# Up product of the feed-forward block: a third one of the seven block products leaves out the two leading columns, and its operand starts 32 columns later in its tile

## The chip, the cores and the metric

The kernel runs on one core of a Trainium2 chip. The metric is the device time of one execution in microseconds (us); lower is better. Times are medians of several runs, and beside them stands one profiled execution, from whose trace all durations of single instructions come. The engines are named as in the profile: PE (TensorE, matrix products), PEld (its weight loads), DVE (VectorE), ACT (ScalarE), POOL (GpSimd), SP (SyncE, which issues most DMAs).

## The reference

One decoder layer on 1040 positions (16 meta tokens and 1024 tokens) of width 1024. After attention, a convolution module and a gated merge, the layer normalises and ends with a convolutional feed-forward block. This block is what the change touches:

```python
h = layer_norm(DEEPNORM_ALPHA * h + mixed @ w_out, ln1_g, ln1_b)
up = causal_dwconv(h @ ffn_w_up, ffn_dw, ffn_dw_b)     # 1024 -> 2 * 2816, then 3 taps along the sequence
u, g = jnp.split(up, 2, axis=-1)
f = (jax.nn.gelu(g, approximate=False) * u) @ ffn_w_down
return layer_norm(DEEPNORM_ALPHA * h + f, ln2_g, ln2_b)
```

The three causal taps need two positions ahead of the first token that is put out. The kernel therefore carries 1026 columns: two leading ones, which are the last two meta tokens, and 1024 tokens.

## The kernel before

All products are float32, made of three matmuls on split operands: `hi*hi`, `hi*lo` and `lo*hi`, where `hi` is the operand cast to the PE's type and `lo` the rest. The stages follow one another: input product and attention, merge, output product with the first layer norm, up product, down product with the second layer norm.

The **up product** `h @ ffn_w_up` works on channels in the partitions and sequence positions in the columns. It is cut into 22 chunks of 128 channels of each of the two halves (up and gate), `for c in range(FC)` at L1473. In a chunk a 2 by 2 block product (two halves of the output channels, two halves of the 1024 inputs; two halves of the sequence) is formed with seven block products in place of eight, in the manner of Strassen and Winograd. The seven right-hand operands B11, B21, BT2, BT1, BT3, BT4, B22 are differences of blocks of `h`. They are formed once, split into `hi` and `lo` by `bsplit` (ACT copy L1188, DVE subtraction L1193), and stay in SBUF for all 22 chunks at the places of `B_AT` (tile, first column). The left-hand operands (weights) are split anew for each chunk by `wsplit` (ACT L1315, DVE L1316, with sums and differences on DVE L1333).

Each operand covers one half of the sequence, 512 tokens and two leading columns: `HW = 514` columns, in two sub-blocks `SUB = [(0, 258), (258, 514)]`. Sub-block 1 has 256 columns. Sub-block 0 has 258, of which the first two are the leading ones. `columns(sub, q)` says which columns a product `q` covers; for sub-block 0, BT3 and B22 begin at column 2. An operand's `hi` and `lo` parts are each four blocks (one per 128 inputs) of that many columns, packed one after the other.

`prod(q, bank, first)` at L1485 issues the matmuls of one product (L1497): for each sub-block, four blocks of inputs by three matmuls, so 12 matmuls of 258 or 256 columns. I call these 12 a group. A chunk has 7 products of two groups, 14 groups. In chunk 0 alone the work goes in two passes, all products of sub-block 1 first, then all of sub-block 0. The order on PE is written out: each product is pinned behind the one before (`last_mm`).

The results go to four PSUM tiles of two banks each: X (`px` in the profile), Z (`pz`), V4 (`pw`) and Y (`py`). The order in a chunk and what empties them:

```python
prod(B11, X, True);  copy(u13[:, a:b], at(X))            # ACT L1509
prod(B21, Z, True);  tt(c11[:, a:b], at(Z), u13[:, a:b], OP.add)   # DVE L1505
prod(BT2, X, False); copy(u2[:, a:b], at(X))
prod(BT4, V4, True)
prod(BT1, Y, True);  copy(c22[:, i:b], at(Y, i))          # i = max(a, 2)
prod(BT3, X, False); copy(u13[:, a:b], at(X))
prod(B22, Y, False); tt(c12[:, i:b], at(Y, i), u2[:, i:b], OP.add)
```

BT1 is thus the product that starts Y, and Y is read only from column `i = 2` on (for its two leading columns c22 and c12 take the last two columns of the other half, by the copy at L1544). Behind the evacuations, DVE and ACT run the three taps (L1422 to L1424), the gelu (L1428) and the gating (L1432), and SP stores the result `fd` to DRAM. In most chunks DVE also forms sums for the down product (`sums_form`, L1455 to L1465).

The **down product** (L1635) is a second seven-product scheme. It loads `fd` and weights, splits them (ACT L1594, DVE L1595), and PE takes them in 42 steps, a pair of 128-row blocks at a time.

The order of instructions on ACT, DVE and SP, where it isn't pinned, is set when the program is built, by a scheduler that works with estimated durations and ranks. So an operand that gets shorter can change that order.

Of the kernel before, what the change touches and what calls it, by code (L numbers as in the profile page):

```python
# [101 lines left out]
def tile_hybrid_layer(  # L102
# [41 lines left out]
    RHC = arena.tile([P, 8320], R, name="RHC")  # L144
    RHO = arena.tile([P, 8320], R, name="RHO")
# [768 lines left out]
    OA = oa_p.tile([P, 8320], R, name="OA")  # L914
# [108 lines left out]
    RX = rx_p.tile([P, 2112], R, name="RX")  # L1023
# [115 lines left out]
    def quadrant(sub, kk, h):  # L1139
# [1 line left out]
        return FA[:, h1_at(sub, i):h1_at(sub, i + 4)]  # L1141


    B_AT = [[(RHC, 6224), (RHO, 4112), (OA, 16), (RX, 16), (OA, 2096), (OA, 6224), (OA, 4144)],
            [(OC, 48), (OC, 2096), (OC, 4144), (OC, 6192), (RHC, 2096), (RHC, 48), (RHC, 4144)]]
    B11, B21, BT2, BT1, BT3, BT4, B22 = range(7)

    def columns(sub, q):

        a, b = SUB[sub]  # L1150
        return (2 if q in (BT3, B22) else a) if sub == 0 else a, b

    def bsum(sub, q, hl):
        a, b = columns(sub, q)
        n = b - a
        t, o = B_AT[sub][q]
        return t[:, o + hl * 4 * n:o + (hl + 1) * 4 * n]

    def bmat(sub, q, hl, k):
        a, b = columns(sub, q)  # L1160
        n = b - a
        return bsum(sub, q, hl)[:, k * n:(k + 1) * n]
# [18 lines left out]
    def bsplit(sub, q, src, cs=slice(None)):  # L1181
        with rank(RK_SUMS):
            a = columns(sub, q)[0] - SUB[sub][0]
            x, y, _ = cs.indices(SUB[sub][1] - SUB[sub][0])
            x = max(x, a)
            hi, lo = (wide(bsum(sub, q, hl))[:, :, x - a:y - a] for hl in range(2))
            src = wide(src)[:, :, x:y]
            ins = nc.scalar.copy(hi, src)  # L1188
            if (sub, q) in ((0, BT2), (0, BT4), (0, BT1), (0, BT3)):
                if high:  # L1190
                    after(ins, high[-1])
                high.append(ins)
            line(nc.vector.tensor_tensor(lo, src, f32(hi), OP.subtract))  # L1193
# [279 lines left out]
    for c in range(FC):  # L1473
        V4, X, Z, Y = (pup.tile([P, 1024], F, name=n, tag=n) for n in ("pw", "px", "pz", "py"))
        passes = ((1,), (0,)) if c == 0 else ((0, 1),)
        for subs in passes:
            last = subs == passes[-1]
            w_next = iter(range(7))
            a, b = SUB[subs[0]][0], SUB[subs[-1]][1]
# [310 lines left out]
```

## Time and profile before

| | us |
|---|---|
| median of 3 runs | 1259.55 |
| lowest and highest run | 1259.47, 1259.66 |
| time of the profiled execution | 1259.33 |
| its span in the trace | 1257.1 |
| first and last start of a matmul of the up product (L1497) | 609.0, about 1039 |
| last matmuls of the down product start | 1248.27 |

The span is the time from the first to the last instruction in the trace; 2.2 us of the profiled execution's time lie around it. In an answer that lists instructions by time, a row has the start, the duration of the stretch (for PE with a modelled end, so that stretches overlap), engine, line, operation, `out<-in`, shape and, behind `x`, how many were merged into the row; in brackets stands the idle time before it and what ended that. The time that a group of 12 matmuls really takes is the distance from its start to the start of the next group.

### The profile page before, as it was taken

Reading aid. Unit: us, or ns where it says so; the run is one execution under the profiler, and the core shown is the slowest. Engines: PE = TensorE matmul, PEld = TensorE weight load, DVE = VectorE, ACT = ScalarE, POOL = GpSimd, SP = SyncE. Lnnn points to the kernel's source line nnn. Section 1 sums busy time; section 2 is a strip of 40 time slices with the busy share of each in tenths; the row PEclk is TensorE's granted clock in tenths of the full one; section 3 lists DMA queues with packets and bytes.
Section 4 is the critical chain, followed back from the end, with each engine's and each line's share of the span. In section 5 each row is a group of like instructions: output and inputs, shape, how many; then the busy total and the mean of one; then the engine's idle time right before and its main releaser. Section 6 shows DMA issues by size and latency. Waiting matters only on the chain.

```text
span 1257.1 us, 21713 instructions
## 1 busy us (share of the span) xinstructions
PE 1246.0 (99%) x8546; PEld 1179.2 (94%) x8546; DVE 1086.6 (86%) x1859; ACT 587.4 (47%) x1057; POOL 54.1 (4%) x28
## 2 busy tenths in 40 slices
PE   9999999999999999999999999999999999999997
PEld 8999999999999999788899999999999998888886
DVE  7899989999989587648899999999999986995697
ACT  7522244545474222335565555554555554544330
POOL 0000000010112132000000000000000000000000
PEclk9999999999999999999999999999999999999999
DMA  7294733332155565222145555463464568998722
GB/s 279 73 309 104 192 95 97 106 94 81 68 141 178 155 171 140 77 75 101 68 134 185 193 210 187 184 218 117 154 230 164 203 211 318 390 328 298 249 86 84
DMA packets 96152, 212.10 MB, mean 169 GB/s; under 512 B 10787, under 2 KB 35939, under 8 KB 95922
## 3 DMA queue, kind: packets, MB, share of 16 engines
q1 hardware_dynamic: 84282, 199.64, 47.4%
q10 hardware_dynamic: 11768, 11.08, 2.7%
q8 instruction: 67, 1.10, 0.4%
q14 instruction: 35, 0.29, 0.1%
HBM read 150.29 MB, written 62.70 MB: 169 GB/s over the span
## 4 chain that ended last, share of the span: by engine, by line
PE 96%; ACT 1%; DVE 1%; DMA 0%; issue 0%; ACTq 0%; DVEq 0%; SPq 0%
PE px L1497 14%; PE py L1497 9%; PE ps_x L1635 9%; PE ps_z L305 8%; PE ps_z L301 8%; PE ps_z L306 8%; PE ps_z L1635 7%; PE pz L1497 5%; PE pw L1497 5%; PE ps_p L306 2%; PE ps_p L301 2%; PE ps_p L305 2%; PE ps_w L306 2%; PE ps_w L301 2%; PE ps_w L305 2%; PE ps_z L517 2%
## 5 line engine op out<-in xcount | busy, mean ns | idle before, releaser
L669 DVE SCALAR_TENSOR_TENSOR FA<-cin,cols,FA 128x1026 f32<-128x1026 f32 x120 | 155.2, 1305 | 0.2
L301 PE MATMUL ps_z<-RHO,whi 128*128 128x384 f32 (+2 forms) x324 | 104.7, 323 | 0.2 <-ACT FA L676 0.2
L305 PE MATMUL ps_z<-RHC,whi 128*128 128x384 f32 (+2 forms) x324 | 104.5, 323 | 0.0
L305 PE MATMUL ps_z<-RHO,whi 128*128 128x384 f32 (+2 forms) x324 | 104.0, 321 | 0.0
L306 PE MATMUL ps_z<-RHC,wlo 128*128 128x384 f32 (+2 forms) x324 | 103.7, 320 | 0.0
L301 PE MATMUL ps_z<-RHC,whi 128*128 128x384 f32 (+2 forms) x324 | 103.7, 320 | 0.0
L306 PE MATMUL ps_z<-RHO,wlo 128*128 128x384 f32 (+2 forms) x324 | 103.4, 319 | 0.0
L1316 DVE TENSOR_TENSOR RHO<-wr,RHO 128x512 fp32r<-128x512 f32 x94 | 63.6, 686 | 5.4 <-ACT RHO L1315 5.4
L1315 ACT CAST RHO<-wr 128x512 fp32r<-128x512 f32 x94 | 56.7, 620 | 24.4 <-DVE wr L1333 11.5
L273 ACT CAST whi<-wr 128x1024 fp32r<-128x1024 f32 x37 | 38.9, 1051 | 56.3 <-PE ps_z L305 31.9
L301 PEld LDWEIGHTS ps_z<-RHO,whi 128*128 128x128 f32 x324 | 60.9, 188 | 0.9 <-ACT FA L676 0.4
L305 PEld LDWEIGHTS ps_z<-RHC,whi 128*128 128x128 f32 x324 | 60.9, 188 | 0.4
L306 PEld LDWEIGHTS ps_z<-RHC,wlo 128*128 128x128 f32 x324 | 60.9, 188 | 0.2
L301 PEld LDWEIGHTS ps_z<-RHC,whi 128*128 128x128 f32 x324 | 60.9, 188 | 0.2
L306 PEld LDWEIGHTS ps_z<-RHO,wlo 128*128 128x128 f32 x324 | 61.0, 188 | 0.1
L305 PEld LDWEIGHTS ps_z<-RHO,whi 128*128 128x128 f32 x324 | 60.9, 188 | 0.1
L1333 DVE TENSOR_TENSOR wr<-wr 128x512 f32<-128x512 f32 x88 | 60.3, 685 | 0.2
L276 POOL TENSOR_TENSOR wlo<-wr,whi 128x1024 fp32r<-128x1024 f32 x17 | 42.3, 2488 | 185.3 <-ACT whi L273 175.7
L676 ACT ACTIVATE FA<-ps_z,cols 128x386 f32<-128x386 f32 (+2 forms) x48 | 26.0, 541 | 46.6 <-PE ps_z L306 39.1
L1509 ACT COPY FA<-px 128x514 f32<-128x514 f32 (+2 forms) x23 | 13.1, 571 | 68.0 <-PE px L1497 67.8
L1316 DVE TENSOR_TENSOR ws<-wr,ws 128x512 fp32r<-128x512 f32 x60 | 40.6, 686 | 4.5 <-ACT ws L1315 4.3
L1422 ACT ACTIVATE FA<-OB,cols 128x512 f32<-128x512 f32 x44 | 35.9, 816 | 14.0 <-DVE OB L1505 14.0
(467 smaller groups left out, 3567.3 us busy)
## 6 DMA issues: line engine op xcount, KB each, us to landing
wr<-in_w_up_dram SPq DMA_DIRECT2D x44, 512.0 KB, 4.6
wr<-in_w_z_dram SPq DMA_DIRECT2D x30, 512.0 KB, 4.0
fd<-FA SPq DMA_DIRECT2D x44, 256.0 KB, 2.5
OB<-in_w_down_dram SPq DMA_DIRECT2D x19, 512.0 KB, 6.2
qt<-qd SPq DMA_DIRECT2D x28, 256.0 KB, 3.7
td<-OB SPq DMA_DIRECT2D x12, 512.0 KB
sums<-fd SPq DMA_DIRECT2D x12, 512.0 KB, 4.8
sd<-sums SPq DMA_DIRECT2D x12, 512.0 KB, 2.7
```

Of the source, the lines that this page charges most:

```text
L273: ins = nc.scalar.copy(hi, raw)
L276: return (nc.vector if quick else nc.gpsimd).tensor_tensor(lo, raw, f32(hi), OP.subtract)
L301: ins = nc.tensor.matmul(ps, ah, bh, start=i == 0, stop=False)
L305: nc.tensor.matmul(ps, ah, bl, start=False, stop=False)
L306: last = nc.tensor.matmul(ps, al, bh, start=False, stop=i == n - 1)
L669: nc.vector.scalar_tensor_tensor(acc[c], cin[:, j:j + U], wc, acc[c], OP.mult, OP.add)
L1315: nc.scalar.copy(hi, src)
L1316: ins = nc.vector.tensor_tensor(lo, src, f32(hi), OP.subtract)
L1333: ins = nc.vector.tensor_tensor(*x)
L1422: nc.scalar.activation(t, cc[:, 2:HW], AF.Identity, bias=ffw(3, o), scale=ffw(2, o))
L1497: ins = nc.tensor.matmul(o, x[:, ks], bmat(sub, q, hl, k), start=first and k + j == 0, stop=k == 3 and j == 2, skip_group_check=not first)
L1635: nc.tensor.matmul(banks[i], l[:, ts], r[:, ws], start=first and a and x + k == 0, stop=z and x == len(ops) - 1 and k == 2, skip_group_che ...
```

## The change

`columns` lets BT1 of sub-block 0 begin at column 2 as BT3 and B22 do, and `B_AT` puts that operand at column 48 of the tile RX in place of column 16.

```diff
-    B_AT = [[(RHC, 6224), (RHO, 4112), (OA, 16), (RX, 16), (OA, 2096), (OA, 6224), (OA, 4144)],
+    B_AT = [[(RHC, 6224), (RHO, 4112), (OA, 16), (RX, 48), (OA, 2096), (OA, 6224), (OA, 4144)],
             [(OC, 48), (OC, 2096), (OC, 4144), (OC, 6192), (RHC, 2096), (RHC, 48), (RHC, 4144)]]
     B11, B21, BT2, BT1, BT3, BT4, B22 = range(7)
 
     def columns(sub, q):
 
         a, b = SUB[sub]
-        return (2 if q in (BT3, B22) else a) if sub == 0 else a, b
+        return (2 if q in (BT1, BT3, B22) else a) if sub == 0 else a, b
```

RX has 2112 columns. The operand took columns 16 to 2079 (8 blocks of 258) and takes columns 48 to 2095 (8 blocks of 256). Its 264 matmuls (12 in each of 22 chunks) have 256 moving columns, the cast and the subtraction that make it have 1024 elements in each partition where they had 1032, and the two columns of Y that nobody reads are no longer written.

## The prediction

> **What bounds the kernel now.** I began with the page: the busy times and the chain of work that ended last.
>
> ```profile
> span 1257.1 us, 21713 instructions
> ...
> PE 1246.0 (99%) x8546; PEld 1179.2 (94%) x8546; DVE 1086.6 (86%) x1859; ACT 587.4 (47%) x1057; POOL 54.1 (4%) x28
> ...
> PE 96%; ACT 1%; DVE 1%; DMA 0%; issue 0%; ACTq 0%; DVEq 0%; SPq 0%
> ```
>
> PE is busy for nearly the whole span and makes up 96% of the chain. Next I asked for the waits of PE, and for the busy times from chunk 1 of the up product to the first matmul of the down product (second answer: stretch, its length, then busy time and instructions of PE, PEld, DVE, ACT, POOL, then the granted clock).
>
> ```profile
> PE px L1497 <- ACT OB L1509: 0.3, 1, 0.3
> ```
>
> ```profile
> 631.95:1039.49 407.54, 407.54 (x3530) 407.54 (x3529) 380.83 (x624) 220.27 (x360) 0.00 (x0) 1.00 0.53 187
> ```
>
> In these 407.54 us PE has no gap and the granted clock is 1.00; its wait for an evacuation lies before them, in chunk 0. So the up product is paced by its own stream of matmuls, and what a group costs is the distance between starts. From the timeline of PE alone, one chunk:
>
> ```profile
> 720.75 1.60 PE L1497 MATMUL py<-RX,RHO 128*128 128x258 f32 x12
> 722.19 1.52 PE L1497 MATMUL py<-OC,RHO 128*128 128x256 f32 x12
> 723.55 1.52 PE L1497 MATMUL px<-OA,RHO 128*128 128x256 f32 x12
> 724.91 1.52 PE L1497 MATMUL px<-RHC,RHO 128*128 128x256 f32 x12
> 726.27 1.52 PE L1497 MATMUL py<-OA,RHO 128*128 128x256 f32 x12
> 727.63 1.52 PE L1497 MATMUL py<-RHC,RHO 128*128 128x256 f32 x12
> 728.99 1.59 PE L1497 MATMUL px<-RHC,RHO 128*128 128x258 f32 x12
> 730.42 1.52 PE L1497 MATMUL px<-OC,RHO 128*128 128x256 f32 x12
> ```
>
> The row at 720.75 is BT1 of sub-block 0, the group that the change touches. From 722.19 to 728.99 stand five groups of 256 columns in 6.80 us, 1.360 each. BT1 took 1.44 by these rounded starts. A finer value comes from the whole stretch: 21 chunks in 407.54 us are 19.407 us each; nine groups of 256 take 12.24 of it, and the five of 258 share 7.167, 1.433 each.
>
> **The change part by part.** *The matmuls.* Two columns go from each of these:
>
> ```profile
> L1497 PE MATMUL py<-RX,RHO x156: 277/282/283, 643.1 to 1032.6; 128*128 128x258 f32 x156
> ...
> L1497 PE MATMUL py<-RX,ws x108: 277/282/283, 627.8 to 1013.2; 128*128 128x258 f32 x108
> ```
>
> 156 and 108 are 264 matmuls, 22 groups. What is a group of BT1 worth afterwards? The nearest rows are the two products that already leave the two columns out, BT3 and B22 of sub-block 0 (723.55 and 726.27): 256 columns, packed one block after the other, 1.360. So a group falls from 1.433 by 0.073 us, and 22 groups by 1.6 us. By the rounded starts of the one row (1.44 against 1.36), or by the modelled lengths (1.60 against 1.52), it would be 1.8. At the low end stands the price of two columns alone, from the down product, whose matmuls have 512:
>
> ```profile
> 1039.49 5.62 PE L1635 MATMUL ps_z<-OC,RHC 128*128 128x512 f32 x24
> 1044.95 5.60 PE L1635 MATMUL ps_z<-OC,RX 128*128 128x512 f32 x24
> 1050.39 5.60 PE L1635 MATMUL ps_z<-OC,RHC 128*128 128x512 f32 x24
> ```
>
> From 1044.95 on 24 of them take 5.44 us, 226.7 ns each; a matmul of 256 takes 113.3 (1.360 over 12). That is 0.443 ns a column, and two columns in 264 matmuls would be 0.23 us. But a matmul of 258 takes 119.4 (1.433 over 12), 6 ns over one of 256 where two columns account for 0.9. The trace puts a price on the length of 258, not on the column, and I take 1.6.
>
> The Trainium skill, in "TensorE: Matmul & The Clock Gate", section "Back-to-back issue gap", gives the distance of two warm matmuls as N / 2.4 + 2.5 ns, which charges each column alone: 109.2 ns for 256 and 110.0 for 258, and the change would then bring an estimated 0.2 us. This trace disagrees for these shapes, with 113.3 and 119.4 ns.
>
> *The place.* No row shows an operand of 256 columns read from RX. Rows that come near: with 258 columns RX costs what RHC costs (1.44 at 720.75, 1.43 at 728.99), so the tile itself isn't slower; and the group at 730.42, B11 of sub-block 1, starts at column 48 of its tile and has the 1.52 of all the others. I price the move at nothing; if the place cost what the two columns cost now, the gain would be zero, and I keep that as the upper bound.
>
> *Making the operand.* Once per execution, in chunk 0, the cast and the subtraction have 1024 elements in place of 1032. Rows of the old form and, for BT3 and B22, of the new one, gaps of two columns in the source included:
>
> ```profile
> 622.52 1.06 ACT L1188 CAST RX<-FA 128x1032 fp32r<-128x1032 f32 x1
> 623.48 1.04 ACT L1188 CAST OA<-FA 128x1024 fp32r<-128x1024 f32 x1
> ```
>
> ```profile
> 625.41 1.23 DVE L1193 TENSOR_TENSOR RX<-FA,RX 128x1032 fp32r<-128x1032 f32 x1
> ...
> 627.15 2.35 DVE L1193 TENSOR_TENSOR OA<-FA,OA 128x1024 fp32r<-128x1024 f32 x2
> ```
>
> That is 0.02 us less on ACT and 0.05 on DVE (2.35 over 2 against 1.23). RX is ready at 626.64 and first read at 627.80 (row further down), so on the path it is worth nothing; without that cover it would be a gain of 0.05 at most.
>
> *What is moved.* The order on PE stays. In the order as built, ACT has five single swaps, in chunks 3 to 14, that put an evacuation (L1509) one place earlier, and a sixth, in chunk 14, that puts one behind a tap activation (L1422). In chunks 14 and 15 some 50 DVE rows and a dozen on ACT stand in another order, and SP has two stores of sums ahead of the two stores of `fd` that they stood between; who waits for those stores is the reuse of eight FA buffers and the load of the next sums on DVE. The last six chunks are ordered as before. No wait, no instruction and no DMA is added. What this order can touch on PE is the handover of PSUM: a bank must be copied before PE's next product on it. The tightest of chunks 1 to 21, and a usual one:
>
> ```profile
> 791.70 0.58 ACT L1509 COPY OB<-px 128x514 f32<-128x514 f32 x1
> ...
> 792.79 1.60 PE L1497 MATMUL px<-OA,ws 128*128 128x258 f32 x12
> ```
>
> ```profile
> 1034.31 0.59 ACT L1509 COPY OB<-py 128x512 f32<-128x512 f32 x1
> ...
> 1036.77 1.52 PE L1497 MATMUL py<-OA,RHO 128*128 128x256 f32 x12
> ```
>
> The leads are 0.51 and 1.87 us. What one or two more instructions ahead of a copy cost, from the page:
>
> ```profile
> L1315 ACT CAST RHO<-wr 128x512 fp32r<-128x512 f32 x94 | 56.7, 620 | 24.4 <-DVE wr L1333 11.5
> ...
> L1422 ACT ACTIVATE FA<-OB,cols 128x512 f32<-128x512 f32 x44 | 35.9, 816 | 14.0 <-DVE OB L1505 14.0
> ```
>
> 0.62 and 0.82 together are 1.44, under the usual lead and 0.93 over the tightest: at most 0.9 in each of chunks 14 and 15, at least nothing. I take nothing.
>
> *The seam to the down product.* PE wants the down operands 1.6 us earlier. Of its 42 steps the one with the smallest lead is step 5, which needs the last chunk's `fd`:
>
> ```profile
> 1064.11 0.69 DVE L1595 TENSOR_TENSOR RHO<-OB,RHO 128x512 fp32r<-128x512 f32 x1 [1.16 <-ACT RHO L1594]
> ...
> 1066.71 1.52 PE L1635 MATMUL ps_z<-RHO,RHC 128*128 128x512 f32 x6
> ```
>
> Ready at 1064.80, used at 1066.71: 1.9 us. Even if that chain stayed where it is, 1.6 fits; and it hangs on the last chunk's results, so it moves along. Behind it PE runs on to the end, and the whole 1.6 us should arrive there.
>
> *Sum.* 1259.33 of the profiled execution less 1.6 is 1257.7; its time stands 0.22 under the median, so the median becomes 1259.55 - 1.6 = **1257.9**, 0.13% faster. As no change counts what lies within 0.2%, 1257.0 to 1262.1, about what a measurement can tell.
>
> **The rivals.** *Column price or place* (gain 0.0 to 0.23): the 6 ns belong to something of BT1 other than its length, its tile or its place in the chunk. For it: nothing has tried RX with 256. Against it: 258 columns cost the same from two tiles. Time 1259.3 to 1259.55.
>
> *The gain stops at the seam*: the down operands, bound by their loads, come as late as before or later, and PE waits for them. For it: that lead of 1.9. Against it: it covers 1.6. Time up to 1259.55.
>
> *The slow pace* (slower). The trace has the very same form at two paces. In chunk 0:
>
> ```profile
> 617.00 1.58 PE L1497 MATMUL py<-OC,ws 128*128 128x256 f32 x12
> 618.42 1.58 PE L1497 MATMUL px<-RHC,ws 128*128 128x256 f32 x12
> 619.83 1.58 PE L1497 MATMUL py<-RHC,ws 128*128 128x256 f32 x12
> ...
> 627.80 1.59 PE L1497 MATMUL py<-RX,ws 128*128 128x258 f32 x12
> 629.24 1.52 PE L1497 MATMUL px<-OA,ws 128*128 128x256 f32 x12
> 630.59 1.52 PE L1497 MATMUL py<-OA,ws 128*128 128x256 f32 x12
> ```
>
> 617.00 to 619.83 is 1.415 a group, against 1.35 at 629.24. I cannot name what ends the slow pace. If the changed mix of lengths kept it up, ten groups of 256 in each of 21 chunks would cost 0.055 more, and a chunk 4 x 1.433 + 10 x 1.415 = 19.88: 0.48 over now, 10 us in all, 1269.5. It decides from some 75 groups on (2.5 us for 0.2%, and the 1.6). Against it: the longest run of 256 in a chunk grows from five groups to seven, and within the five no pace changes.
>
> *Larger than summed*: the four other products of 258 columns fall to 1.36 too, because neighbours share what costs 0.073: 88 groups, 6.4 us more, 1251.5. Against it: the row at 728.99 costs 1.43 with groups of 256 on both sides.
>
> *Handover* (slower): the copy comes 0.3 us late in each of 21 chunks (0.82 against the lead of 0.51), 6.3 less 1.6: 1264.3. Five of the six swaps speak against it.
>
> **How the numbers follow.** Forecast 70%; column price or place 6%, seam 4%: these are "same", 80%. Larger 10% is "faster". Slow pace 6% and handover 4% are "slower", 10%. The range reaches from 1257.4 (a gain of 1.8, and 0.2 more each way for the scatter of the runs) to 1259.6 (no gain) and leaves out the last three cases.
>
> **What would show it.** After the change `py<-RX` has 128x256 and its successor starts 1.36 later; a chunk takes 19.33 us; chunk 1 to the first L1635 takes 406.0; PE shows no new wait at L1497 or L1635; from that L1635 to the end it stays 217.6. Wrong would be: a BT1 group over 1.40, groups of 256 at 1.41 in chunks 1 to 21, a wait of PE for L1509, or a down product that grows by what the up product gained.

## The result, and the profile after

| | before | after |
|---|---|---|
| median (22 runs each, same chip), us | 1259.41 | 1257.75 |
| lowest and highest, us | 1259.00, 1259.95 | 1257.46, 1258.85 |
| span of the profiled execution, us | 1257.1 | 1255.5 |
| first matmul of the down product, us | 1039.49 | 1037.93 |

The ratio is 0.9987, with a 95% interval of 0.9981 to 0.9993: 1.66 us less, where 1.6 were forecast. The interval lies below 1, so the gain is clear of the noise; by the prediction's bound of 0.2% it counts as no change.

From the page of the changed kernel, the busy times and the chain that ended last:

```profile
span 1255.5 us, 21717 instructions
...
PE 1244.1 (99%) x8546; PEld 1177.3 (94%) x8546; DVE 1086.5 (87%) x1859; ACT 586.6 (47%) x1057; POOL 54.0 (4%) x28
...
PE 96%; ACT 1%; DVE 1%; DMA 1%; issue 0%; SPq 0%; ACTq 0%; DVEq 0%
```

PE lost 1.9 us of busy time and is still the bound. Next, the waits of PE in the changed kernel (total, times, longest), and its busy times (columns as before) from chunk 1 to the first matmul of the down product and from there to the end:

```profile
PE px L1497 <- ACT OB L1509: 0.4, 1, 0.4
```

```profile
631.93:1037.93 406.00, 406.00 (x3530) 406.00 (x3529) 380.73 (x624) 219.71 (x360) 0.00 (x0) 1.00 0.53 187
1037.93:1255.50 217.57, 209.62 (x926) 173.24 (x924) 172.22 (x247) 81.55 (x92) 0.00 (x0) 0.99 0.69 249
```

The stretch of 21 chunks took 407.54 us and takes 406.00; PE has no gap in it. The down product takes 217.6 as before. So the whole gain is made in the up product and arrives at the end. The timeline of PE in one chunk of the changed kernel:

```profile
701.10 1.52 PE L1497 MATMUL py<-RX,RHO 128*128 128x256 f32 x12
702.46 1.52 PE L1497 MATMUL py<-OC,RHO 128*128 128x256 f32 x12
703.82 1.52 PE L1497 MATMUL px<-OA,RHO 128*128 128x256 f32 x12
705.18 1.52 PE L1497 MATMUL px<-RHC,RHO 128*128 128x256 f32 x12
```

The BT1 group now has 128x256 and its successor starts 1.36 later. Durations of groups are from here on distances of starts in the trace to the nanosecond, in us: BT1 went from 1.434 to 1.360 in each of the 22 chunks, and in chunks 1 to 21 no other group changed by more than 0.001.

So far the sum stands. The diff, however, makes two edits at once, and the prediction gave the whole gain to one of them, the length. The experiments take them apart.

### The profile page after: what moved, and what is told of

It is laid out like the page before. It is cut to its first block, busy times and chain, and to the rows that moved or that the text cites. A ratio compares the mean times of both kernels' runs of the same rounds, so it can differ in the third digit from the quotient of the medians.

```text
span 1255.5 us, 21717 instructions
## 1 busy us (share of the span) xinstructions
PE 1244.1 (99%) x8546; PEld 1177.3 (94%) x8546; DVE 1086.5 (87%) x1859; ACT 586.6 (47%) x1057; POOL 54.0 (4%) x28
## 4 chain that ended last, share of the span: by engine, by line
PE 96%; ACT 1%; DVE 1%; DMA 1%; issue 0%; SPq 0%; ACTq 0%; DVEq 0%
PE px L1497 14%; PE py L1497 9%; PE ps_x L1635 9%; PE ps_z L305 8%; PE ps_z L301 8%; PE ps_z L306 8%; PE ps_z L1635 7%; PE pz L1497 5%; PE pw L1497 5%; PE ps_p L306 2%; PE ps_p L301 2%; PE ps_p L305 2%; PE ps_w L301 2%; PE ps_w L306 2%; PE ps_w L305 2%; PE ps_z L517 2%
## 5 line engine op out<-in xcount | busy, mean ns | idle before, releaser
L1509 ACT COPY FA<-px 128x514 f32<-128x514 f32 (+2 forms) x23 | 13.1, 570 | 70.5 <-PE px L1497 70.5
```

## The experiments

### Each edit alone

Four kernels. w256_at16 has the new length at the old place, w258_at48 the old length at the new place, w256_at18 the new length at the place where the old operand's third column lay. b22_258 is the kernel before with the two leading columns put back into another product, B22 of sub-block 0.

```diff
 w256_at16, against the changed kernel
-(RX, 48)
+(RX, 16)
 w256_at18, against the changed kernel
-(RX, 48)
+(RX, 18)
 w258_at48, against the kernel before
-(RX, 16)
+(RX, 48)
 b22_258, against the kernel before
-        return (2 if q in (BT3, B22) else a) if sub == 0 else a, b
+        return (2 if q in (BT3,) else a) if sub == 0 else a, b
```

> The new width with the old start: BT1 of sub-block 0 has 256 columns, its operand begins at column 16 of RX again. If the width alone carries the gain (my theory), a BT1 group stays at 1.360 us and the time at 1257.75. If the new start carries it (rival: place), the group is back at 1.43 and the time at 1259.4.

> The new start with the old width: 258 columns from column 48 of RX. Width theory: a BT1 group takes 1.433 us, the time is that of before, 1259.4. Place theory: 1.36 a group and 1257.8.

> 256 columns, but the operand begins at column 18 of RX, 8 bytes behind a multiple of 16 columns. Theory A (the price hangs on the number of columns): 1.360 us a group, 1257.75. Theory B (the operand is read in stretches of 16 columns, 64 bytes, and what counts is how many of them a row of the operand touches; 258 columns touch 17, and so do 256 that begin 2 columns late): 17 x 7.08 ns = 120.4 ns a matmul, 1.445 a group, the whole gain lost, 1259.5.

> The kernel before, and B22 of sub-block 0 given the two leading columns too (258 columns, nobody reads what the two give). If the price belongs to any product of 258 columns, a B22 group rises from 1.360 to 1.433 and the time by 1.6 us to 1261.0. If it belongs to BT1's place in the chunk or to its tile, nothing changes: 1259.4.

Measured, against 27 runs of the kernel before on the same chip (median 1259.28):

| | median us | ratio, 95% interval | BT1 group |
|---|---|---|---|
| w256_at16 | 1259.23 | 0.9999 (0.9990 to 1.0007) | 1.413 |
| w256_at18 | 1260.23 | 1.0009 (1.0000 to 1.0018) | 1.443 |
| w258_at48 | 1265.27 | 1.0049 (1.0036 to 1.0062) | 1.433 |
| b22_258 | 1262.09 | 1.0023 (1.0014 to 1.0032) | 1.434 (B22: 1.432) |

The timeline of PE in w256_at16:

```profile
701.59 1.57 PE L1497 MATMUL py<-RX,RHO 128*128 128x256 f32 x12
703.00 1.53 PE L1497 MATMUL py<-OC,RHO 128*128 128x256 f32 x12
704.37 1.52 PE L1497 MATMUL px<-OA,RHO 128*128 128x256 f32 x12
705.73 1.52 PE L1497 MATMUL px<-RHC,RHO 128*128 128x256 f32 x12
```

256 columns, and yet the successor starts 1.41 later, and the group behind it takes 1.367. Against 258 columns the shorter length alone gains 0.021 in BT1 and loses 0.007 behind it: 0.014 x 22 = 0.3 us by the rows, too little for the medians to show. The same 256 columns from column 48 gain 0.053 and 0.007 more, 1.3 us. From column 18 they take 1.443, more than 258 columns from 16. That is close to the 1.445 of theory B; but by theory B columns 16 and 48 would cost the same, and they differ by 0.053. Now the timeline of PE in w258_at48, the other edit alone:

```profile
702.59 1.60 PE L1497 MATMUL py<-RX,RHO 128*128 128x258 f32 x12
704.02 1.58 PE L1497 MATMUL py<-OC,RHO 128*128 128x256 f32 x12
705.43 1.58 PE L1497 MATMUL px<-OA,RHO 128*128 128x256 f32 x12
706.85 1.58 PE L1497 MATMUL px<-RHC,RHO 128*128 128x256 f32 x12
708.26 1.58 PE L1497 MATMUL py<-OA,ws 128*128 128x256 f32 x12
709.67 1.58 PE L1497 MATMUL py<-RHC,ws 128*128 128x256 f32 x12
711.09 1.60 PE L1497 MATMUL px<-RHC,ws 128*128 128x258 f32 x12
712.53 1.52 PE L1497 MATMUL px<-OC,ws 128*128 128x256 f32 x12
```

The moved group itself takes 1.433, next to the 1.434 of before. The loss stands behind it: five groups that nobody edited go from 1.360 to 1.413-1.416, until the next group of 258 ends it. Five times 0.054 and 0.006 in that next group, in 22 chunks, is 6.1 us; 6.0 were measured. It is the pace that the prediction met in chunk 0 and could not name; here one group hands it on. Every engine runs its instructions in the order of the kernel before, so the order has no part in it.

b22_258 does the same in another tile: its operand, too, lies at a column that is 48 beyond a multiple of 64 (4144). The group of 258 costs 0.072 more, the one behind it runs at 1.416 in place of 1.360 and B11 at 1.439 in place of 1.434, together 0.133 x 22 = 2.9; 2.8 were measured.

Column numbers modulo 64 (64 columns are 256 bytes) then put the table `B_AT` in order: of the kernel before, every operand of 258 columns starts at 16 (6224, 4112, 16, 16, 6224), and every one of 256 at 48 (48, 2096, 4144, 6192). With 256 columns all eight blocks of an operand start at the same place, with 258 each block starts 2 columns further on. The change takes BT1's operand from one class to the other in both respects.

### Fewer columns, and other neighbours

If a matmul is paid by the column, or in stretches of 16, reading only 240 must pay, and 242 tells the two apart. cut242 and cut240 are the changed kernel with 11 of the 12 matmuls of BT1 cut short; two_passes gives chunk 1 the two passes of chunk 0, to see if the order of products makes the slow pace.

```diff
 cut242 (cut240 with 240)
+    CUT = 242
...
+                            rhs = bmat(sub, q, hl, k)
+                            if (sub, q) == (0, BT1) and k + j:
+                                o, rhs = bank[:, 256:256 + CUT], rhs[:, 0:CUT]
 two_passes
-        passes = ((1,), (0,)) if c == 0 else ((0, 1),)
+        passes = ((1,), (0,)) if c < 2 else ((0, 1),)
...
-            if not last:
+            if not last and c == 0:
```

> The changed kernel, in which 11 of the 12 matmuls of each BT1 group of sub-block 0 take 242 columns only (the last 14 columns of the product are left out). If each column has its price (0.443 ns), such a matmul takes 107.1 ns, a group 1.292 us in place of 1.360. If columns count in stretches of 16 (242 touch 16 of them, as 256 do), it stays at 113.3 ns and 1.360.

> As the run with 242, with 240 columns (15 stretches of 16; the last 16 columns of the product are left out). Both theories: 106.2 ns a matmul, 1.282 us a group. Against the run with 242 columns: 0.01 us less a group if columns count singly, 0.078 less if they count in stretches of 16.

> The changed kernel with chunk 1 in two passes as chunk 0 has them, all products of sub-block 1 first. Tests the slow pace of chunk 0's first pass (1.415 us for a group of 256 columns). If it comes from products of one sub-block following each other, chunk 1's first pass takes 1.41 to 1.42 a group too; if it comes from what else goes on at that time in chunk 0, chunk 1's first pass takes 1.36.

Measured against 8 runs of the kernel before (1259.5): cut242 1265.37, ratio 1.0044 (1.0028 to 1.0061); cut240 1263.32, 1.0032 (1.0019 to 1.0045); two_passes 1259.83 in one run. Fewer columns made the kernel slower than the one before, and by 7.6 and 5.6 us slower than the changed one (1257.75 on another chip). The timeline of PE in cut240 (its matmuls of the up product are at L1501):

```profile
703.02 1.51 PE L1501 MATMUL py<-RX,RHO 128*128 128x256 f32 x12
704.36 1.58 PE L1501 MATMUL py<-OC,RHO 128*128 128x256 f32 x12
705.78 1.58 PE L1501 MATMUL px<-OA,RHO 128*128 128x256 f32 x12
...
710.02 1.58 PE L1501 MATMUL py<-RHC,ws 128*128 128x256 f32 x12
711.43 1.58 PE L1501 MATMUL px<-RHC,ws 128*128 128x258 f32 x12
712.85 1.52 PE L1501 MATMUL px<-OC,ws 128*128 128x256 f32 x12
```

The cut group (named by its first matmul, which keeps 256) takes 1.342, where by the column it would take 1.282; cut242 takes 1.359, next to the 1.360 of 256 columns. Both hand the slow pace to the five groups behind, cut242 also to the one behind the next group of 258 (1.413). So neither a price by the column nor one by stretches holds, and an operation can be shortened and lose.

The timeline of PE in two_passes, around the passes of chunks 0 and 1:

```profile
609.37 1.58 PE L1497 MATMUL px<-OC,RHO 128*128 128x256 f32 x12
610.78 1.58 PE L1497 MATMUL pz<-OC,RHO 128*128 128x256 f32 x12
...
615.80 1.68 PE L1497 MATMUL pw<-RHC,RHO 128*128 128x256 f32 x12 [0.97 <-ACT FA L1298]
...
632.00 1.52 PE L1497 MATMUL px<-OC,ws 128*128 128x256 f32 x12
633.36 1.52 PE L1497 MATMUL pz<-OC,RHO 128*128 128x256 f32 x12
634.72 0.39 PE L1497 MATMUL px<-OC,RHO 128*128 128x256 f32 x2
635.81 1.40 PE L1497 MATMUL px<-OC,RHO 128*128 128x256 f32 x10 [0.70 <-DVE RHO L1316]
637.05 1.52 PE L1497 MATMUL pw<-RHC,RHO 128*128 128x256 f32 x12
638.41 1.52 PE L1497 MATMUL py<-OC,RHO 128*128 128x256 f32 x12
```

The same products in the same order, 1.41 a group in chunk 0 and 1.36 in chunk 1, there on both sides of a stall. In chunk 0, too, the slow pace stands on both sides of a stall, the wait of 0.97 ahead of 615.80 (the groups at 610.78 and 617.32 take 1.413 each). So the order of products alone doesn't make the slow pace. Whether chunk 0 has it from what ran before or from what else runs at that time, this run doesn't tell. The 0.3 us over the kernel before is no test of this: the second early pass brought stalls of its own.

### Nine starts, and other lengths

One kernel tries 21 forms of the BT1 group, one in each chunk from 1 on, so each form is one group: first column, distance of the blocks, columns read.

```diff
+    TRY = [(0, 256, 256), (8, 256, 256), (16, 256, 256), (24, 256, 256), (32, 256, 256), (40, 256, 256), (48, 256, 256),
+           (56, 256, 256), (64, 256, 256), (0, 258, 258), (16, 258, 258), (32, 258, 258), (48, 258, 258),
+           (0, 256, 258), (16, 256, 258), (32, 256, 258), (48, 256, 258), (0, 264, 258), (0, 264, 264),
+           (16, 256, 272), (48, 256, 272)]
...
+                            if (sub, q) == (0, BT1) and c:
+                                s, t, n = TRY[c - 1]
+                                rhs = RX[:, s + (hl * 4 + k) * t:s + (hl * 4 + k) * t + n]
+                                o = bank[:, 512 - n:512]
```

> One kernel with 21 forms: in chunks 1 to 21 the 12 matmuls of BT1, sub-block 0, read RX from another start column, at another distance of the blocks or with another number of columns (what the product then gives is not BT1's; its operand lies at column 64). Chunks 1 to 9: 256 columns, blocks 256 apart, starts 0, 8, 16, 24, 32, 40, 48, 56, 64. Column 16 of RX is a multiple of 256 bytes. Theory S1 (the start within 256 bytes decides): 48 alone takes 1.360 us a group, the others 1.41 to 1.45, and 16 repeats 1.413. Theory S2 (any start on a multiple of 16 columns is as good, 16 was slow for another reason): 0, 16, 32, 48, 64 are equal. Chunks 10 to 17: 258 columns with blocks 258 or 256 apart. If the price of 258 is that of ragged block starts, those 256 apart fall to about 1.37; if it is that of the length, all stay near 1.43. Chunks 18 to 21: 258 and 264 at distance 264, 272 at distance 256: in stretches of 16 columns 272 costs what 258 does, 1.43 to 1.45; by single columns 1.445. Beside each, the pace of the next five groups of 256 shows whether it hands on the fast pace (1.360) or the slow one (1.414).

Its one run took 1262.81 us (before 1259.93), a sum over all forms; the rows count here. The BT1 group with 256 columns, and what it hands on, by the first column:

| first column | BT1 group | behind it |
|---|---|---|
| 0, 64 | 1.421 | one group of 1.379, then 1.360 |
| 8 | 1.403 | 1.377, then 1.360 |
| 16 | 1.414 | 1.366, then 1.360 |
| 24 | 1.426 | 1.380, then 1.360 |
| 32 | 1.428 | 1.385, then 1.360 |
| 40 | 1.409 | five groups of 1.413 |
| **48** | **1.360** | 1.360 |
| 56 | 1.414 | five groups of 1.414 |

The timeline of PE shows three of these rows, for the first columns 40, 48 and 56 (L1506 in this kernel):

```profile
741.17 1.57 PE L1506 MATMUL py<-RX,ws 128*128 128x256 f32 x12
742.58 1.58 PE L1506 MATMUL py<-OC,ws 128*128 128x256 f32 x12
...
760.83 1.52 PE L1506 MATMUL py<-RX,RHO 128*128 128x256 f32 x12
762.19 1.52 PE L1506 MATMUL py<-OC,RHO 128*128 128x256 f32 x12
...
780.16 1.58 PE L1506 MATMUL py<-RX,RHO 128*128 128x256 f32 x12
781.58 1.58 PE L1506 MATMUL py<-OC,RHO 128*128 128x256 f32 x12
```

Of nine starts only 48, the one in the change, keeps the pace of 1.360; 0 and 64 agree, as a period of 64 columns would have it. With 258 columns the group takes 1.433 to 1.469 whatever its start or its blocks' distance, so blocks that begin at uneven columns are not its price. Packed at 258 it hands on the fast pace from 0, 16 and 32 and the slow one from 48; with blocks 256 apart it hands on the fast one from 16 and 48 and the slow one from 0 and 32. So for 258 columns the first column alone doesn't decide what is handed on. 264 columns take 1.459, and 272 take 1.48 to 1.52, more than either theory gave; all three hand on the slow pace. No form of 258 came near 1.360, so nothing here promises a gain from moving the four other products of 258 columns.

### The other operand

Why 48? In the up product all operands of 256 start there, and the weights in RHO start at multiples of 64 columns (0 and 6208, and 1024 apart). If what counts is the place of the moving operand against the weights, moving the weights must hurt as much. weights_16 moves four of the ten slots that hold the weights by 16 columns; they overwrite 16 columns of the output product's operand that is still read, so that part of that product is changed and also has to wait. weights_ws16 moves two slots that nobody else uses. z_on_64 is an attempt to use the finding: the 384-column blocks of the input product's operand start at 48 modulo 64.

```diff
 weights_16, against the changed kernel
-    RING = [RHO[:, i * 1024:(i + 1) * 1024] for i in range(4)]
+    RING = [RHO[:, 16 + i * 1024:16 + (i + 1) * 1024] for i in range(4)]
 weights_ws16, against the changed kernel
-            RING[i] = wsp("ws", ("whi", "wlo")[i % 2])[:, 0:D]
+            RING[i] = wsp("ws", ("whi", "wlo")[i % 2])[:, 16 * (i % 2):16 * (i % 2) + D]
 z_on_64, against the changed kernel
-ZG = [(0, 400), (400, 784), (784, 1040)]
+ZG = [(0, 272), (272, 656), (656, 1040)]
...
     def h0(k, hl, a, b):
-        o = ((k % 4) * 2 + hl) * T
+        g = max(i for i in range(3) if HG[i][0] <= a)
+        c, d = HG[g]
+        o = (0, 2224, 5296)[g] + ((k % 4) * 2 + hl) * (d - c) - c
...
-        return tmp_p.tile([P, 386], F, name="t", tag="t", bufs=6)[:, :n]
+        return tmp_p.tile([P, 386], F, name="t", tag="t", bufs=5)[:, :n]
```

> The changed kernel, in which four of the ten slots that hold the split weights of the up product (the first four in RHO) begin 16 columns, 64 bytes, later. The moving operands stay where they are. Theory M (the place of the moving operand alone decides the pace): all groups keep 1.360 and 1.434 us, 1257.7. Theory R (what counts is where the moving operand lies against the weights): the groups with weights from these slots, some 88 of 256 columns, leave the fast pace (1.41 or more), 4 to 6 us in all, about 1262 to 1264.

> The changed kernel; two of the ten slots of split weights (the second and the fourth that are named ws) begin 16 columns, 64 bytes, later, in room that nothing else uses. Theory R (the moving operand's place against the weights' sets the pace): groups of 256 with weights from these two slots leave 1.360 for 1.41 to 1.43; some 30 products in all, with what they hand on 2 to 4 us, 1259.8 to 1261.8. Theory M (the moving operand's place alone): all groups as in the changed kernel, 1257.75.

> The changed kernel, and the finding about start columns carried to the input product (L301 to L306 in stage z): its moving operand is laid out in three pieces of 272, 384 and 384 columns, so that all blocks of 384 start at the place within 256 bytes that is fast in the up product (128), and the stage works in these pieces in place of 400, 384 and 256; one buffer of six less in the convolution's norm makes the room. If the rule holds for 384 columns, such a matmul takes 170 ns (384 x 0.443) in place of about 176, and the product some 6 to 8 us less in all: 1250 to 1252. If the rule belongs to 256 columns alone, the time stays within 2 us of 1257.75.

weights_16 took 1275.96 in its one run (before 1259.31), and 12.2 us of that stand ahead of the up product, which begins at 621.2 in place of 609.05. More than half of them is a wait in the output product's stage, by the waits of PE:

```profile
PE ps_h L1285 <- DVE OB L1275: 7.2, 2, 3.6
```

The granted clock also fell there, to 0.94 from 540.00 to 621.20, where the changed kernel has 1.00 up to its up product. The up product alone, at 1.00 again, took 434.9 us against 428.9, 6.0 more, with the groups of 256 on moved weights at 1.417 to 1.430. weights_ws16 has no such side effect: 1261.08, ratio 1.0014 (1.0004 to 1.0023) to a kernel before of 1259.47, so 1.6 over before and some 3.3 over the changed kernel. Its up product, and that of the changed kernel, in busy times:

```profile
609.19:1041.21 432.02, 430.65 (x3706) 429.82 (x3704) 401.72 (x660) 234.76 (x389) 0.00 (x0) 1.00 0.52 180
```

```profile
609.05:1037.93 428.88, 427.55 (x3705) 426.71 (x3704) 401.86 (x659) 234.56 (x389) 0.00 (x0) 1.00 0.51 181
```

And the timeline of PE in weights_ws16, where moved weights begin at 682.16 and unmoved ones at 685.00:

```profile
680.79 1.52 PE L1497 MATMUL pw<-RHC,RHO 128*128 128x256 f32 x12
682.16 1.58 PE L1497 MATMUL py<-RX,ws 128*128 128x256 f32 x12
683.58 1.58 PE L1497 MATMUL py<-OC,ws 128*128 128x256 f32 x12
685.00 1.54 PE L1497 MATMUL px<-OA,ws 128*128 128x256 f32 x12
686.37 1.52 PE L1497 MATMUL px<-RHC,ws 128*128 128x256 f32 x12
```

The same moving operand at column 48 now costs 1.42. So column 48 isn't good by itself: where the weights lie counts as well. In chunks 1 to 21 all 41 groups of 256 on moved weights take 1.418 to 1.429. The 17 groups of 258 on them go the other way: 1.417 to 1.418, where those on unmoved weights take 1.430 to 1.440.

z_on_64 gained nothing: 1261.32, ratio 1.0015 (1.0005 to 1.0025), 3.6 over the changed kernel and outside both expectations. Its matmuls of 384 columns stand 176.7 ns apart on average where it was 176.2 (medians 174 and 175), and new waits of PE came ahead of the up product, 1.8 us the longest; that the buffer less brought them is likely, not shown. So the first column that is good in the up product isn't good as such in another stage; whether that stage's weights are the reason wasn't tried.

The last run moves both: operand and weights 16 columns later.

```diff
 both_shifted, against weights_ws16
-(RX, 48)
+(RX, 64)
```

> weights_ws16 with the operand of BT1 sub-block 0 at column 64 of RX in place of 48: operand and, in every second slot of the ws tiles, weights are both 16 columns later than in the changed kernel. Four BT1 groups use such shifted weights (those that began at 682.16, 798.96, 876.99 and 993.80 in weights_ws16, 1.418 to 1.420 each there); the other 18 use weights that are not shifted. Theory of the distance (what counts is where the moving operand lies relative to the weights): the four shifted groups fall to 1.360 (up to 1.37 for the two behind a slow group), while the other BT1 groups rise from 1.360 to 1.42, as start 64 did in the run starts, and the group behind them to 1.38. Rival, places of their own (operand and weights each have good places, whatever the other does): the four stay at 1.41 or more, and the 18 rise as well. The total is near 1262.3 by both (18 x 0.08 more, four x 0.06 less or nothing less), so the rows decide, not the time.

It took 1262.03 in its one run (before 1259.5). The 18 groups on unmoved weights rose to 1.42 to 1.44, and those behind to 1.38, as both theories had it. Of the four on moved weights, those at 682.50 and 877.69 took 1.410 and those at 799.72 and 994.91 took 1.385; neither theory expected this split. The timeline of PE around the first and the second:

```profile
681.13 1.52 PE L1497 MATMUL pw<-RHC,RHO 128*128 128x256 f32 x12
682.50 1.57 PE L1497 MATMUL py<-RX,ws 128*128 128x256 f32 x12
683.91 1.61 PE L1497 MATMUL py<-OC,ws 128*128 128x256 f32 x12
...
798.29 1.59 PE L1497 MATMUL pw<-RHC,ws 128*128 128x256 f32 x12
799.72 1.55 PE L1497 MATMUL py<-RX,ws 128*128 128x256 f32 x12
801.10 1.59 PE L1497 MATMUL py<-OC,ws 128*128 128x256 f32 x12
```

The distances of the 12 single matmuls in ns say more:

```
682.50  114 118 118 117 118 118 117 119 117 118 118 118
799.72  115 120 115 123 118 114 113 113 114 113 113 114
```

With both moved, the stream settles: at 682.50 on 118, the slow pace, and at 799.72 on 113, the fast one. With only one moved it settles on neither: the weights_ws16 group at 682.16 goes on between 115 and 124 behind its first four matmuls, and an operand at 64 on unmoved weights between 116 and 124 behind its first two. So moving both brings back the two settled paces, but the relative place alone doesn't choose between them.

What stood before the group differs as well. The two that settle on 118 follow a group on unmoved weights (681.13, 1.364), the two that settle on 113 a group on moved ones (798.29, 1.429). So what a group meets may take part in the choice; with four groups in one run that is not shown. Neither theory's numbers hold for all four: the distance gave 1.360 to 1.37, which none of them met, and the rival 1.41 or more, which two met. Only the return of settled paces speaks for the distance.

## Why the prediction was right, and which step wasn't

- *What bounds it*: right. PE without a gap, the same chain, the same granted clock.
- *The matmuls*: 1.434 to 1.360 in 22 groups, 1.6 us: right to a nanosecond a group. The reason given was wrong in part. "The trace puts a price on the length of 258" holds at the new place only; at the old one the two columns are worth 0.3 us (w256_at16). That is near the 0.23 of the price by the column, which the prediction kept as its low end. The Trainium skill's rule of 2.4 columns per ns and a constant ("TensorE: Matmul & The Clock Gate", "Back-to-back issue gap"), which the page gives for a matmul by itself and not for a stream of pairs of weight load and matmul as this is, gives an estimated 0.2 for the length. The trace agrees with that difference at column 16 and not with the rest: 240 columns take 1.6 ns less than 256 (1.342 against 1.360, over the 11 that were cut) where the rule has 6.7, and 256 columns take 113 or 118 ns by where they lie.
- *The place*: this step failed. "I price the move at nothing": measured, the move is worth 1.3 us to the operand of 256 and costs 6.0 us with one of 258. That the total came out right was luck: the rows used as price, BT3 and B22, lie at column 48 modulo 64 themselves (2096 and 4144), so 1.360 already had the place in it. The prediction named the column of one row, 730.42, and otherwise compared tiles and shapes; it did not set the columns of BT3 and B22 in `B_AT` beside the 16 that BT1 had. The rival "column price or place" got 6% for a reason that was real: with the operand at column 16 it would have come true.
- *The slow pace*: it did not come, as forecast, but the mechanism exists and one column number in a table brings it: 6.0 us in w258_at48. The prediction's argument against it, that within five groups of 256 no pace changes, holds for this layout alone. Its trigger was looked for in the mix of lengths; the runs show that length, start, distance of the blocks and the weights' place all bear on it.
- *Making the operand, what is moved*: nothing, as priced: PE's wait for L1509 grew from 0.3 to 0.4, in chunk 0, and no wait joined it in chunks 1 to 21. "No wait, no instruction" was not exact: the trace has 21717 instructions where it had 21713, all of the difference semaphore instructions, most of them on DVE, and they cost PE nothing. w256_at16 keeps the changed kernel's order of instructions on every engine and still loses nearly the whole gain, so the order is not what made it.
- *The seam*: right. In the changed kernel, the last split that step 5 needs (timeline of DVE), and its use (timeline of PE):

```profile
1062.40 0.69 DVE L1595 TENSOR_TENSOR RHO<-OB,RHO 128x512 fp32r<-128x512 f32 x1 [0.89 <-ACT RHO L1594]
```

```profile
1065.14 2.20 PE L1635 MATMUL ps_z<-RHO,RHC 128*128 128x512 f32 x9
```

  Ready at 1063.09, used at 1065.14: the lead is 2.05 us where it was 1.91. The chain moved along, as argued.
- *Larger than summed, handover*: neither came; the other products of 258 kept 1.434.
- *The range*: its ends don't follow from the terms named for them. 1259.55 less 1.8 and 0.2 is 1257.55, not 1257.4, and no gain with 0.2 of scatter is 1259.75, not 1259.6. The measured 1257.75 lies within either.

Open: what in TensorE's reads makes the place count, why a settled pace goes over to later groups, what sets it in chunk 0, why 258 columns packed at 258 hand on the fast pace from column 16 and the slow one from 48, and what chooses the pace when operand and weights are both moved. The runs show that each happens, not why. None of the kernels run beat the changed one.

## What to carry to other kernels

When PE is the bound and its operands are packed by hand, list first column and length of every moving operand, and the place of its weights, modulo 256 bytes; a new operand goes where the fast ones of the same length lie, and its price is taken from a row that agrees in place as well as in shape. Read the groups behind an edited one too, since the cost can fall on them. An edit of two parts that meets its forecast is still to be taken apart: here one part alone was worth 0.3 us by its rows, the other alone cost 6.0, and both together gained 1.6.

## What was not expected of the hardware

- The same form, 256 moving columns, has two settled paces at a granted clock of 1.00: 113.3 and 117.8 ns a matmul, 4% apart. A pace is handed from group to group (w258_at48), and in two_passes each of the two stands on both sides of a stall.
- Moving the weights by 64 bytes slows matmuls of 256 columns as moving the operand does (weights_ws16, 1.360 to 1.42), and makes those of 258 faster (1.434 to 1.417). The Trainium skill ("TensorE: Matmul & The Clock Gate", "Step-by-step: what each phase is for") gives weight loads a read port of their own, so that loading the next weights takes no bandwidth from the running matmul. No run here measures bandwidth; but in a stream of pairs as it is here, one load to each matmul, the loads are not without effect: the place of the weights shows in the time of the matmuls.
- Reading fewer columns can cost time: with 240 in place of 256 in one group of 14 the kernel took 1263.32 us, 5.6 more than the changed one (cut240). The cut group gained 0.018 and the five behind it lost 0.053 each.
